# Block 1's attention with its projections in pieces of six matmuls between steps of heads, and values two steps later

## The chip, the cores and the metric

The kernel runs on one core of a Trainium2 chip. The time is in device microseconds (us), the median of several runs. Five engines work side by side and wait for each other through semaphores: TensorE (PE in the profile; its weight loads are PEld), VectorE (DVE), ScalarE (ACT), GpSimd (POOL) and SyncE (SP), whose queue issues most of the DMAs. Each engine works through its own instructions in the order in which the program issues them; that order is fixed when the program is built.

## The reference

Three blocks follow each other on x, 512 tokens by 1024 features. The change is in the first block's token mixing (`first_block`). All of it is float32.

```python
h = rms_norm(x, mix_norm)
qa, ka, va, qb, kb, vb = split(h @ w_in)      # 512, 512, 512, 512, 128, 128 columns
# 8 differential heads, each with two queries and two keys of 32, a value of 64
p  = softmax(q1 @ k1.T * scale + bias) - lam * softmax(q2 @ k2.T * scale + bias)
oa = rms_norm(p @ va, diff_subln) * (1 - lambda_init)
# 8 grouped heads of 64; 4 share a key and a value
qb, kb = rope(rms_norm(qb, q_norm)), rope(rms_norm(kb, k_norm))
ob = softmax(qb @ kb.T * 64 ** -0.5) @ vb
x  = x + concat(oa, ob) @ w_out
```

## The kernel before, in words

**Layout.** Activations stand feature-major: a chunk is 128 features (partitions) by 512 tokens. float32 products are made from three matmuls of fp32r operands: each operand is split into a high part and a low part, and high by high, low by high and high by low are accumulated (lines 120 to 122, `mm3x`). A projection onto one chunk sums over eight input chunks, so it is 24 matmuls of 128x512. Its weight arrives by DMA (`wraw`, line 169); ACT makes the high part (`whi`, line 137) and DVE, or POOL where `pool_lo` is set, the low part (`wlo`, line 138).

**Banks.** The eight PSUM banks are letters a to h. Scores use a and b, transposed weights of the softmax c and d, outputs e and f; small sums and turns use g ("st"), and a projection made during the heads uses h ("pj").

**The attention (`heads1`, from line 563).** There are four q chunks and four k chunks of the differential heads, four q chunks and one k chunk (called chunk 4) of the grouped heads. A q or k chunk is scaled out of its bank (`af`, line 607), split by ACT and DVE into one buffer `hl` (`parts`, lines 488 to 500; `HL` is the number of its buffers), and written to DRAM (line 499: `qdd`, `kdd`, `qpd`, `kpd`). The operands of a head are then loaded back from there in the row order that a score matmul needs (`qd` and `kd`, line 614; `qg`, line 690; `kg`, line 598). The grouped ones go through a norm and rope first (`rope`, lines 569 to 591): sums over features on PE, small operations of DVE, a rotation on ACT and POOL (lines 583 to 585), a copy `hr` of the norm on POOL (line 242), which PE turns into bank g (line 247), and a product on DVE.

**Values.** `v_tokens` (line 505) makes all values at once with tokens on the partitions: 192 matmuls of 128x320 in four banks, c to f.

**Heads.** Sixteen heads are run in the order differential, grouped, differential, grouped, with two of each per chunk. `attend` emits, for each of four chunks of 128 queries of a head, the scores (two matmuls for the two softmaxes, line 627, or two that add up, line 651), the softmax (a biased minimum or a minimum on DVE, lines 629 and 652; an exponential on ACT, line 485), the sum of the two softmaxes (lines 635 to 641; chunks 0 and 2 on POOL, lines 638 and 639), and the values of the *previous* head (`values`: four transposes, line 462, a split by ACT and DVE, lines 470 and 471, two matmuls, lines 472 and 473).

**What sets the order.** Before the heads stand seven projections (k chunk 4 of the grouped heads; q, k and grouped q of chunks 0 and 1) and the values. When a head's first score is built (`lazy`, `mk_diff`, `mk_gqa`), the projections and operand loads that belong there are emitted. Engine priority is by emission, and `issue_after(x)` holds an instruction behind x. `half_res` adds the first half of the output projection, eight pieces of twelve matmuls, held behind marks of the last heads (`M0`, `M1`); after the attention comes the other half.

Of the kernel before, what the change touches and what calls it, by code (L numbers as in the profile page):

```python
# [29 lines left out]
def f32v(ap):  # L30
    return ap.bitcast(F32)


class K:
    NU = 5
    SECOND = ("dq", "pf", "ct", "cacc")
    out = "out"
    NL = 4
    AH = 2
    HL = 1  # L40
# [14 lines left out]
    BANKS = {"mm": "abcdef", "scores": "ab", "abh": "abh", "e": "e", "fh": "fh", "turned": "cd", "out": "ef", "pj": "h", "cdef": "cdef", "st": "g", "bg": "h", "abcd": "abcd", "ef": "ef"}  # L55
# [375 lines left out]
    def attend(self, heads):  # L431

        nc = self.nc
        pv, self.marks = None, []
        for unit, vt, odd, dst, done in heads + [(None,) * 5]:
            ps_, fin = [], None
            for q in range(4):
                f = unit(q) if unit else None  # L440
                if fin:
                    ps_.append(fin())
                fin = f
                if pv:
                    self.values(pv, q)
            if fin:
                ps_.append(fin())
            if pv:
                self.fold(pv[0], pv[3], pv[4])
                if pv[5]:  # L450
                    pv[5]()
            pv = [None, ps_, vt, odd, dst, done] if unit else None
# [52 lines left out]
    def v_tokens(self, src, xhl, vt, rtok, nh):  # L505

        nc = self.nc
        for half in range(2):
            pv = [self.psum("cdef") for _ in range(4)]
            for k0, kn in ((0, 3), (3, 3), (6, 2)):  # L510
                W = self.weight(src[half][:, k0 * 320:(k0 + kn) * 320], kn * 320, kn)
                for q in range(4):
                    s = slice(q * 128, (q + 1) * 128)
                    self.mm3x(pv[q][:, :320], [(xhl[k0 + k][0][:, s], xhl[k0 + k][1][:, s]) + W[k] for k in range(kn)], k0 == 0, k0 == 6)
            for q in range(4):
                hv = vt[q][:, half * 5:half * 5 + 5]
                pvv = pv[q][:, :320].rearrange("p (h d) -> p h d", h=5)
                nc.scalar.activation(hv[:, :, 0:64], pvv, AF.Copy, scale=rtok[:, q:q + 1])
                nc.vector.scalar_tensor_tensor(out=hv[:, :, 64:128], in0=pvv, scalar=rtok[:, q:q + 1], in1=f32v(hv[:, :, 0:64]), op0=ALU.mult, op1=ALU.subtract)

    def mix1(self, inp, gnext):
# [7 lines left out]
        with self.phase("att"):  # L529
            self.heads1(xhl, rb, rtok, gq, ind, ocs)  # L530
            part = self.half_res(ocs, gs, res)
# [15 lines left out]
    def half_res(self, ocs, gs, res):  # L547

        nc, D = self.nc, self.D
        ohl = self.o_parts(ocs, gs, (0, 4, 1, 5), "x", 16)  # L550
        part = self.dr.tile([8, 128, 512], F32, name="part")
        for c in range(8):
            x = self.keep("xa", 3)
            nc.sync.dma_start(out=x, in_=res[c])
            self.pool_lo = self.PA
            with self.tc.issue_after(self.marks[32 + self.M0 + self.M1 * c // 8]):
                p = self.proj(D["w_out"][c][:, :512], ohl, 4, "pj")
            self.pool_lo = False
            nc.vector.tensor_add(x, p, x)
            nc.sync.dma_start(out=part[c], in_=x)  # L560
        return part

    def heads1(self, xhl, rb, rtok, gq, ind, ocs):
# [5 lines left out]
        def rope(c, name, kind="pj"):  # L569
# [5 lines left out]
            nc.vector.tensor_mul(f0, self.proj(D["w1_in"][8 + c], xhl, kind=kind), rb)  # L575
# [13 lines left out]
            return self.parts(f, name)  # L589

        d = rope(4, "kpd", "mm")

        def keys(kv):
            ds = []
            for i in range(2):
                t = self.keep("kg", 2, F32R)
                for r in range(2):
                    nc.sync.dma_start(out=f32v(t[64 * r:64 * r + 64]), in_=self.part_rows(d, i, 32 * kv, [(64, 2), (1, 32)]))
# [18 lines left out]
        def diff_head(h, sms, q2, k2):  # L617
# [4 lines left out]
            def unit(q):  # L622
                mx = self.small("mx", 2, 4)
                es = []
                for s in range(2):
                    p = self.psum("scores")
                    nc.tensor.matmul(p, q2[:96, s, q * 128:(q + 1) * 128], k2[:96, s], start=True, stop=True)
# [29 lines left out]
        qds, kds, qgd = {}, {}, {}  # L657
# [10 lines left out]
        def proj_q(c, kind="pj"):  # L668
            qds[c] = scaled("qdd", self.proj(D["w1_in"][c], xhl, kind=kind), -(32 ** -0.5))

        def proj_k(c, kind="pj"):
            kds[c] = scaled("kdd", self.proj(D["w1_in"][4 + c], xhl, kind=kind), 1.0)

        def mk_diff(c, r):
            if r == 1:
                qgd[c + self.AH] = rope(c + self.AH, "qpd") if c < 4 - self.AH else None
# [1434 lines left out]
```

## Time and profile before

| what | us |
|---|---|
| median of 3 runs (2668.03, 2668.23, 2671.92) | 2668.23 |
| profiled execution | 2667.55 |
| its span, first to last instruction | 2665.6 |
| attention stage, from the sixth projection's end (422.83) to the output projection's second half (671.90) | 249.07 |
| first score matmul | 450.24 |

The profile is of one execution. Its mean granted TensorE clock is 0.989 of full speed. In the table of engines a busy time and its share stand with the number of instructions. In the views by windows each row is a stretch of the span in us, with the busy time of each engine and the number of its instructions. In timelines a row has start, duration, engine, line, operation, output <- inputs, and in brackets the idle time ahead of the instruction with what ended it. Matmuls are pipelined, so that the distance of two starts, not the duration, is what one costs.

### The profile page before, as it was taken

What the parts mean: (1) busy time and instruction counts of PE and PEld (TensorE: products, weight loads), DVE (VectorE), ACT (ScalarE), POOL (GpSimd) and SP (SyncE); (2) the same over time, 40 slices, a digit from 0 to 9 for tenths busy, and PEclk for the clock granted to TensorE, in tenths of its full rate; (3) what the DMA queues carried; (4) which work ended last, traced back from release to release, by engine and by line L of the source; (5) the groups of instructions that cost most, each with busy time, mean ns of one, the idle gap of its engine ahead of it and who ended that gap; (6) DMA issues with size and microseconds to landing.
All of it is one profiled execution on the core that took longest, in us unless ns stands there. A gap on an engine that the chain in (4) does not pass through costs nothing.

```text
span 2665.6 us, 31162 instructions
## 1 busy us (share of the span) xinstructions
PE 2590.5 (97%) x11804; PEld 2093.0 (79%) x11804; DVE 1580.7 (59%) x2446; ACT 1052.8 (39%) x1621; POOL 405.0 (15%) x331
## 2 busy tenths in 40 slices
PE   8999998989999999999999999999899899999999
PEld 6887787767788887988788777888788777878787
DVE  7876645888644544567435854334545976746564
ACT  4222233776422324555323533223433463424242
POOL 1011012233000003133112201001200313101000
PEclk9999999999999999999999999999999999999999
DMA  5565644433632234432223343222524644322323
GB/s 197 179 200 189 212 154 128 152 111 103 208 96 96 87 103 134 143 106 70 97 95 134 127 144 99 95 95 95 186 70 147 211 103 156 95 94 91 100 87 111
DMA packets 114593, 339.99 MB, mean 128 GB/s; under 512 B 13784, under 2 KB 15768, under 8 KB 114314
## 3 DMA queue, kind: packets, MB, share of 16 engines
q1 hardware_dynamic: 104010, 301.02, 34.6%
q0 software_dynamic: 10432, 36.97, 4.4%
q8 instruction: 92, 1.51, 0.2%
q14 instruction: 59, 0.48, 0.1%
HBM read 301.47 MB, written 40.67 MB: 128 GB/s over the span
## 4 chain that ended last, share of the span: by engine, by line
PE 78%; issue 8%; DVE 6%; DMA 4%; ACT 2%; POOL 1%; SPq 0%; POOLq 0%; ACTq 0%; DVEq 0%
PE a L121 4%; PE a L120 4%; PE a L122 4%; PE e L122 4%; PE c L122 4%; PE c L121 4%; PE c L120 4%; PE e L120 4%; PE e L121 4%; PE b L122 4%; PE f L120 4%; PE f L121 4%; PE b L120 4%; PE b L121 4%; PE f L122 4%
## 5 line engine op out<-in xcount | busy, mean ns | idle before, releaser
L137 ACT ACTIVATE whi<-wraw 128x1024 fp32r<-128x1024 f32 (+4 forms) x420 | 423.9, 1012 | 1024.9 <-PE e L121 169.6
L138 DVE TENSOR_TENSOR wlo<-wraw,whi 128x1024 fp32r<-128x1024 f32 (+5 forms) x408 | 492.3, 1209 | 323.1 <-ACT whi L137 317.4
L122 PE MATMUL e<-xh,wlo 128*128 128x512 f32 x368 | 144.0, 391 | 1.6 <-DVE wlo L138 1.6
L120 PE MATMUL e<-xh,whi 128*128 128x512 f32 x368 | 144.2, 392 | 0.0
L121 PE MATMUL e<-xl,whi 128*128 128x512 f32 x368 | 144.1, 392 | 0.0
L121 PE MATMUL a<-xl,whi 128*128 128x512 f32 x352 | 139.2, 396 | 2.4 <-DVE xl L194 2.0
L120 PE MATMUL a<-xh,whi 128*128 128x512 f32 x352 | 138.9, 395 | 0.2 <-ACT xh L897 0.2
L122 PE MATMUL a<-xh,wlo 128*128 128x512 f32 x352 | 138.1, 392 | 0.1
L121 PE MATMUL c<-xl,whi 128*128 128x512 f32 x344 | 135.3, 393 | 2.5 <-DVE xl L194 2.5
L120 PE MATMUL c<-xh,whi 128*128 128x512 f32 x344 | 135.7, 394 | 0.0
L122 PE MATMUL c<-xh,wlo 128*128 128x512 f32 x344 | 135.1, 393 | 0.0
L120 PE MATMUL b<-xh,whi 128*128 128x512 f32 x304 | 120.2, 395 | 10.1 <-ACT xh L193 7.7
L121 PE MATMUL b<-xl,whi 128*128 128x512 f32 x304 | 120.2, 395 | 0.0
L122 PE MATMUL b<-xh,wlo 128*128 128x512 f32 x304 | 119.8, 394 | 0.3 <-DVE wlo L138 0.3
L190 ACT ACTIVATE hh<-h 128x512 fp32r<-128x512 f32 x98 | 61.8, 630 | 144.6 <-DVE h L369 93.0
L928 POOL TENSOR_TENSOR acc<-sq 128x512 f32<-128x512 f32 x10 | 14.1, 1406 | 638.3 <-ACT sq L296 371.8
L122 PE MATMUL f<-xh,wlo 128*128 128x512 f32 x280 | 109.8, 392 | 0.6 <-DVE wlo L138 0.6
L120 PE MATMUL f<-xh,whi 128*128 128x512 f32 x280 | 110.2, 394 | 0.0
L121 PE MATMUL f<-xl,whi 128*128 128x512 f32 x280 | 109.4, 391 | 0.0
L122 PE MATMUL d<-xh,wlo 128*128 128x512 f32 x264 | 104.2, 395 | 1.6 <-DVE wlo L138 1.6
L120 PE MATMUL d<-xh,whi 128*128 128x512 f32 x264 | 104.3, 395 | 0.0
L121 PE MATMUL d<-xl,whi 128*128 128x512 f32 x264 | 103.7, 393 | 0.0
(1181 smaller groups left out, 6447.2 us busy)
## 6 DMA issues: line engine op xcount, KB each, us to landing
wraw<-w_up SPq DMA_DIRECT2D x76, 512.0 KB
mw<-w_mod POOLq DMA_DIRECT2D x48, 512.0 KB, 4.6
wraw<-ffn_w_gate SPq DMA_DIRECT2D x43, 512.0 KB
wraw<-ffn_w_up SPq DMA_DIRECT2D x43, 512.0 KB
wraw<-w_down SPq DMA_DIRECT2D x40, 512.0 KB
wraw<-ffn_w_down SPq DMA_DIRECT2D x32, 448.0 KB
wraw<-w_gate SPq DMA_DIRECT2D x24, 512.0 KB
wraw<-ffn_w_down SPq DMA_DIRECT2D x16, 512.0 KB
```

Source lines behind the costliest of these rows:

```text
L120: mm(out, ah, bh, start=(first and i == 0), stop=False)
L121: mm(out, ah, bl, start=False, stop=False)
L122: self.last_mm = mm(out, al, bh, start=False, stop=(last and i == n - 1)).ins
L137: nc.scalar.activation(hi[:, i:j], raw[:, i:j], AF.Copy)
L138: (nc.gpsimd if self.pool_lo else nc.vector).tensor_sub(lo[:, i:j], raw[:, i:j], f32v(hi[:, i:j]))
L190: nc.scalar.activation(hi, x, AF.Copy)
L928: i = (self.nc.vector if c == 6 else self.nc.gpsimd).tensor_add(a, acc, s).ins
```

## The change

`attend` is given `fill`, a generator, and `lag`. It emits in steps: one query chunk of one head (scores, softmax), then the values of the chunk that was emitted 4 + `lag` steps earlier (`lag` is 2 here, so six steps; before, four), then one piece of `fill`. A piece is six matmuls: two of the eight input chunks of a projection (`proj_pieces`). A projection takes four steps. `fill` goes through chunks 1 to 3, each with grouped q (rope), q, k and v, and then through the first half of the output projection (two pieces each).

Values are now four chunks and a fifth for the grouped heads, made feature-major like every other projection; each is scaled on DVE, turned by four PE transposes into bank g and split there (`turn_v`).

Ahead of the heads stand six projections: q0, k0, grouped q 0, chunk 4, v0 and v4. The loads of the first head's operands come right behind k0. Operands of a head are loaded one head ahead (`ahead_diff`, `ahead_gqa`). There are two `hl` buffers, four operand buffers in place of three, and three of `kg` in place of two. `pool_lo` is set for all of `fill`, so that POOL makes the low parts of its twelve full weights too. The third block's attention uses the same `attend` without fill and lag, with its own counter of score banks.

```diff
-    AH = 2
-    HL = 1
+    HL = 2
...
-    M0 = 4
-    M1 = 30
-    PA = True
...
+    def attend(self, heads, fill=None, lag=0):
+
+
+
+
+        n, pvs, fin, self.marks = len(heads), [], None, []
+        for step in range(4 * n + 4 + lag):
+            f, (h, q) = None, divmod(step, 4)
+            if h < n:
+                unit, vt, odd, dst, done = heads[h]
+                if q == 0:
+                    pvs.append([None, [], vt, odd, dst, done])
+                f = unit(q)
...
+                fin[0].append(fin[1]())
+            fin = (pvs[h][1], f) if f else None
+            h, kc = divmod(step - 4 - lag, 4)
+            if h >= 0:
+                pv = pvs[h]
+                self.values(pv, kc)
+                if kc == 3:
+                    self.fold(pv[0], pv[3], pv[4])
+                    if pv[5]:
+                        pv[5]()
+            if fill:
+                with self.tc.issue_after(self.marks[-1] if self.marks else self.last_score):
+                    next(fill, None)
...
+    def proj_pieces(self, src, xhl, evac, kind="pj"):
+
+        W = self.weight(src, 1024, 8)
+        p = self.psum(kind)
+        for k in range(0, 8, 2):
+            self.mm3x(p, [W[k] + xhl[k], W[k + 1] + xhl[k + 1]], k == 0, k == 6)
+            if k == 6:
+                evac(p)
+            yield
...
-            self.pool_lo = self.PA
-            with self.tc.issue_after(self.marks[32 + self.M0 + self.M1 * c // 8]):
-                p = self.proj(D["w_out"][c][:, :512], ohl, 4, "pj")
...
+            W = self.weight(D["w_out"][c][:, :512], 512, 4)
+            p = self.psum("pj")
+            for k in range(0, 4, 2):
+                self.mm3x(p, [W[k] + ohl[k], W[k + 1] + ohl[k + 1]], k == 0, k == 2)
+                if k == 2:
+                    nc.vector.tensor_add(x, p, x)
+                    nc.sync.dma_start(out=part[c], in_=x)
+                yield
...
-                t = self.keep("kg", 2, F32R)
+                t = self.keep("kg", 3, F32R)
...
-        vt = [self.keep("vt", 4, F32R, w=1280).rearrange("p (h d) -> p h d", h=10) for _ in range(4)]
...
+        vt = [self.keep("vt", 5, F32R, w=1024).rearrange("p (q h d) -> p q h d", q=4, h=2) for _ in range(5)]
+
+        def turn_v(p, c):
+            f = self.t("vf")
+            nc.vector.tensor_mul(f, p, rb)
+            p = self.psum("st")
+            for q in range(4):
+                nc.tensor.transpose(p[:, q * 128:q * 128 + 128], f[:, q * 128:q * 128 + 128], self.ident)
+            p = p.rearrange("p (q h d) -> p q h d", q=4, h=2)
+            nc.scalar.activation(vt[c][:, :, :, 0:64], p, AF.Copy)
+            nc.vector.tensor_sub(vt[c][:, :, :, 64:128], p, f32v(vt[c][:, :, :, 0:64]))
...
-            t = self.keep(tag, 3, F32R, tag="op1", w=1024).rearrange("p (r w) -> p r w", r=2)
+            t = self.keep(tag, 4, F32R, tag="op1", w=1024).rearrange("p (r w) -> p r w", r=2)
...
-                    nc.tensor.matmul(p, q2[:96, s, q * 128:(q + 1) * 128], k2[:96, s], start=True, stop=True)
+                    self.last_score = nc.tensor.matmul(p, q2[:96, s, q * 128:(q + 1) * 128], k2[:96, s], start=True, stop=True).ins
...
+        def chunk(kind, c):
+
+            return {"q": (D["w1_in"][c], lambda p: scaled(qds, c, "qdd", p, -(32 ** -0.5))),
+                    "k": (D["w1_in"][4 + c], lambda p: scaled(kds, c, "kdd", p, 1.0)),
+                    "g": (D["w1_in"][8 + c], lambda p: rope(p, c)),
+                    "v": (D["w1_v"][c], lambda p: turn_v(p, c))}[kind]
+
+        def ahead_diff(c, r):
+
+            ops[c, r] = operand("qd", qds[c], r, (0, 0, 1)), operand("kd", kds[c], r, (0, 1, 0))
+
+        def ahead_gqa(c, r):
+            if r == 0 and c % 2 == 0:
+                kg[c // 2] = keys(c // 2)
...
+            ops[4 + c, r] = t
+
+        def mk_diff(c, r):
+            ahead_gqa(c, r)
+            return diff_head(2 * c + r, sms[c], *ops[c, r])
+
+        def mk_gqa(c, r):
+            if (c, r) != (3, 1):
+                ahead_diff(c + r, 1 - r)
+            return gqa_head(r, sms[4 + c], ops[4 + c, r], kg[c // 2])
...
-        for c in range(self.AH):
-            proj_q(c, "mm")
-            proj_k(c, "mm")
-            qgd[c] = rope(c, "qpd", "mm")
+        for kind, c in (("q", 0), ("k", 0), ("g", 0), ("g", 4), ("v", 0), ("v", 4)):
+            src, evac = chunk(kind, c)
+            evac(self.proj(src, xhl))
+            if kind == "k":
+                ahead_diff(0, 0)
+
+        def fill():
+            self.pool_lo = True
+            for c in range(1, 4):
+                for kind in "gqkv":
+                    yield from self.proj_pieces(*chunk(kind, c)[:1], xhl, chunk(kind, c)[1])
+            yield from rest()
+            self.pool_lo = False
...
-        self.attend(heads)
+                heads.append((lazy(lambda c=c, r=r: mk_diff(c, r)), [vt[c][:, q, r] for q in range(4)], r, ocs[c], normed(c) if r else None))
+                heads.append((lazy(lambda c=c, r=r: mk_gqa(c, r)), [vt[4][:, q, h // 4] for q in range(4)], r, ocs[4 + c], normed(4 + c) if r else None))
+        self.attend(heads, fill(), 2)
...
-    A["w1_v"] = moving(np.concatenate([w[:, 1024:1536], w[:, 2176:]], 1), 320)
+    A["w1_v"] = panels(np.concatenate([w[:, 1024:1536], w[:, 2176:]], 1))
```

**PE, at the start of the scores.** Rows of PE's order, of before; `kd` and `qd` are the operands of the first differential head, `f_3459` a bank of the values (the fourth of the first half), `c_3456` to `e_3458` the three others. Words in a row are the line, the operation, output<-inputs and the shape.

```order
L122 MATMUL f_3459<-whi_3462,xl_2750 128x320
L120 MATMUL f_3459<-whi_3504,xh_2788 128x320
L121 MATMUL f_3459<-wlo_3505,xh_2788 128x320
L122 MATMUL f_3459<-whi_3504,xl_2789 128x320
L120 MATMUL f_3459<-whi_3504,xh_2827 128x320
L627 MATMUL a_3395<-kd_3388,qd_3384 128x512
L220 MATMUL g_3343<-vecs_74,sq_3344 128x2 x4
L627 MATMUL b_3400<-kd_3388,qd_3384 128x512
L121 MATMUL f_3459<-wlo_3505,xh_2827 128x320
L122 MATMUL f_3459<-whi_3504,xl_2828 128x320
L120 MATMUL f_3459<-whi_3504,xh_2866 128x320
L121 MATMUL f_3459<-wlo_3505,xh_2866 128x320
```

The same place in the changed kernel: `f_3290` is the sixth projection (v4), `h_3352` the first piece of grouped q of chunk 1. The lines have moved with the edits: 120 to 122 are 116 to 118 now, 242 is 238, 462 is 463, 499 is 500, 614 is 618, 627 is 631, 638 and 639 are 642 and 643.

```order
L117 MATMUL f_3290<-xl_2945,whi_3286 128x512
L118 MATMUL f_3290<-xh_2944,wlo_3287 128x512
L631 MATMUL a_3336<-kd_3092,qd_3088 128x512
L631 MATMUL b_3341<-kd_3092,qd_3088 128x512
L116 MATMUL h_3352<-xh_2673,whi_3348 128x512
L117 MATMUL h_3352<-xl_2674,whi_3348 128x512
L118 MATMUL h_3352<-xh_2673,wlo_3349 128x512
L116 MATMUL h_3352<-xh_2710,whi_3348 128x512
L117 MATMUL h_3352<-xl_2711,whi_3348 128x512
L118 MATMUL h_3352<-xh_2710,wlo_3349 128x512
L631 MATMUL a_3360<-kd_3092,qd_3088 128x512
L631 MATMUL b_3365<-kd_3092,qd_3088 128x512
```

Scores now stand directly behind the last of six projections, with one piece of six matmuls between two steps; before, they stood among the value matmuls, behind seven projections and most of the first half of the values.

**POOL, around the first grouped head.** Of before: `rot` and `hr` belong to rope, `e1` to the sums of two softmaxes.

```order
L242 COPY hr_3219<-rr_3203 128x4x64 x2
L584 TENSOR_TENSOR rot_3364<-rot_3364,rope_2996 128x512
L585 TENSOR_TENSOR rot_3364<-ra_3362,rot_3364 128x512
L242 COPY hr_3369<-rr_3353 128x4x64 x2
L638 TENSOR_SCALAR e1_3402<-e1_3402,rs_3416 128x512
L639 TENSOR_TENSOR e1_3402<-e1_3402,e0_3397 128x512
L638 TENSOR_SCALAR e1_3429<-e1_3429,rs_3447 128x512
L639 TENSOR_TENSOR e1_3429<-e1_3429,e0_3424 128x512
L638 TENSOR_SCALAR e1_3958<-e1_3958,rs_3984 128x512
L639 TENSOR_TENSOR e1_3958<-e1_3958,e0_3953 128x512
```

Of the changed kernel: `e1_3343` and `e1_3389` are the sums of chunks 0 and 2 of the first head, `wlo_3598` the low half of the weight of k of chunk 1, `hr_3229` the norm of the grouped keys (chunk 4).

```order
L580 TENSOR_TENSOR rot_3224<-rot_3224,rope_2997 128x512
L581 TENSOR_TENSOR rot_3224<-ra_3222,rot_3224 128x512
L642 TENSOR_SCALAR e1_3343<-e1_3343,rs_3370 128x512
L643 TENSOR_TENSOR e1_3343<-e1_3343,e0_3338 128x512
L642 TENSOR_SCALAR e1_3389<-e1_3389,rs_3413 128x512
L134 TENSOR_TENSOR wlo_3598<-wraw_3595,whi_3597 128x1024
L238 COPY hr_3229<-rr_3213 128x4x64 x2
L643 TENSOR_TENSOR e1_3389<-e1_3389,e0_3384 128x512
L580 TENSOR_TENSOR rot_3447<-rot_3447,rope_2997 128x512
L581 TENSOR_TENSOR rot_3447<-ra_3445,rot_3447 128x512
```

The low half now stands between two halves of a head's work and the copy of the grouped keys' norm. This is where PE stands in the changed kernel at that place (`c_3520` and `d_3544` are the transposed weights of the first head's values, `g_3232` the turned norm, `g_3277` the turned v4):

```order
L117 MATMUL h_3352<-xl_2945,whi_3348 128x512
L118 MATMUL h_3352<-xh_2944,wlo_3349 128x512
L463 MATMUL c_3520<-ident_72,e1_3343 128x128
L463 MATMUL c_3520<-ident_72,e1_3367 128x128
L463 MATMUL d_3544<-ident_72,e1_3343 128x128
L463 MATMUL d_3544<-ident_72,e1_3367 128x128
L243 MATMUL g_3232<-ident_72,hr_3229 128x128 x4
L463 MATMUL c_3520<-ident_72,e1_3389 128x128
L463 MATMUL c_3520<-ident_72,e1_3410 128x128
L463 MATMUL d_3544<-ident_72,e1_3389 128x128
L463 MATMUL d_3544<-ident_72,e1_3410 128x128
L604 MATMUL g_3277<-ident_72,vf_3275 128x128 x4
```

PE needs `e1_3343`, then `hr_3229`, then `e1_3389`, in the order in which POOL makes them, with the low half ahead of `hr_3229`.

**SP's queue, at a change of chunk.** Of before, from the write of k of chunk 2 (`kdd_3788`) on; its first load stands seven rows below the last one shown:

```order
L499 DMA kdd_3788<-hl_3785 128x1024
L169 DMA wraw_5722<-w_out 128x512
L614 DMA kd_4172<-kdd_3308 32x2x512 x3
L614 DMA qd_4523<-qdd_3270 32x2x512 x3
L620 DMA btab_4531<-be2_2029 128x896
L169 DMA wraw_5745<-w_out 128x512
L690 DMA qg_4640<-qpd_3382 64x1x512 x2
L499 DMA qpd_3938<-hl_3935 128x1024
L614 DMA kd_4527<-kdd_3308 32x2x512 x3
L614 DMA qd_4751<-qdd_3750 32x2x512 x3
```

Of the changed kernel, the change from chunk 1 to chunk 2 (`kdd_4335` is the write of k of chunk 2, `kd_4341` the load of its first half for the head that follows):

```order
L500 DMA qpd_4054<-hl_4051 128x1024
L500 DMA qdd_4189<-hl_4186 128x1024
L688 DMA qg_4468<-qpd_4054 64x1x512 x2
L618 DMA qd_4337<-qdd_4189 32x2x512 x3
L624 DMA btab_4823<-be2_2029 128x896
L500 DMA kdd_4335<-hl_4332 128x1024
L165 DMA wraw_4996<-w1_v 128x1024
L618 DMA kd_4341<-kdd_4335 32x2x512 x3
L618 DMA qd_4685<-qdd_4189 32x2x512 x3
L592 DMA kg_4465<-kpd_3242 64x1x512 x2
L618 DMA kd_4689<-kdd_4335 32x2x512 x3
```

The write of the keys and their load now stand one behind the other with a weight load between them; before, writes stood several rows ahead of the loads that need them.

More of the change, by code (lines that the diff above doesn't have):

```diff
@@ L54 @@
     NW = 3
-    BANKS = {"mm": "abcdef", "scores": "ab", "abh": "abh", "e": "e", "fh": "fh", "turned": "cd", "out": "ef", "pj": "h", "cdef": "cdef", "st": "g", "bg": "h", "abcd": "abcd", "ef": "ef"}
+    BANKS = {"mm": "abcdef", "scores": "ab", "scores3": "ab", "abh": "abh", "e": "e", "fh": "fh", "turned": "cd", "out": "ef", "pj": "h", "cdef": "cdef", "st": "g", "bg": "h", "abcd": "abcd", "ef": "ef"}
     def __init__(self, ctx, tc, D):
@@ L503, in part_rows @@
         return bass.AP(tensor=d.tensor, offset=d.offset + row * 1024 + part * 512, ap=[[s * 1024, n] for s, n in dims] + [[1, 512]])
[L505 to L519, printed above, removed]
+    def proj_pieces(self, src, xhl, evac, kind="pj"):
[6 more added lines that the diff above has]
+            yield
     def mix1(self, inp, gnext):
@@ L529, in mix1 @@
         with self.phase("att"):
-            self.heads1(xhl, rb, rtok, gq, ind, ocs)
-            part = self.half_res(ocs, gs, res)
+            part = self.dr.tile([8, 128, 512], F32, name="part")
+            self.heads1(xhl, rb, gq, ind, ocs, lambda: self.half_res(ocs, gs, res, part))
         with self.phase("wo"):
@@ L554, in half_res, with heads1 @@
             nc.sync.dma_start(out=x, in_=res[c])
-            self.pool_lo = self.PA
-            with self.tc.issue_after(self.marks[32 + self.M0 + self.M1 * c // 8]):
-                p = self.proj(D["w_out"][c][:, :512], ohl, 4, "pj")
[L558 to L563, printed above, removed]
+            W = self.weight(D["w_out"][c][:, :512], 512, 4)
[6 more added lines that the diff above has]
+                yield
+    def heads1(self, xhl, rb, gq, ind, ocs, rest):
         nc, D = self.nc, self.D
@@ L567, in heads1, with rope @@
         nc.sync.dma_start(out=cs, in_=D["rope1"])
-        def rope(c, name, kind="pj"):
+        def rope(p, c):
             i = int(c == 4)
             f0 = self.t("rf0")
-            nc.vector.tensor_mul(f0, self.proj(D["w1_in"][8 + c], xhl, kind=kind), rb)
+            nc.vector.tensor_mul(f0, p, rb)
             st = self.psum("st")
@@ L588, in rope @@
             nc.vector.scalar_tensor_tensor(out=f, in0=p, scalar=1.0 if c == 4 else -0.125, in1=rot, op0=ALU.mult, op1=ALU.mult)
-            return self.parts(f, name)
-        d = rope(4, "kpd", "mm")
+            gds[c] = self.parts(f, "kpd" if c == 4 else "qpd")
         def keys(kv):
@@ L655, in gqa_head @@
             return unit
-        qds, kds, qgd = {}, {}, {}
+        qds, kds, gds, ops = {}, {}, {}, {}
         def lazy(mk):
@@ L666, in lazy @@
             return unit
[L668 to L676, printed above, removed]
-            return diff_head(2 * c + r, sms[c], operand("qd", qds[c], r, (0, 0, 1)), operand("kd", kds[c], r, (0, 1, 0)))
-        def mk_gqa(c, r):
-            if r == 0:
-                if c == 0:
-                    self.v_tokens(D["w1_v"], xhl, vt, rtok, 5)
-                if c % 2 == 0:
-                    kg[c // 2] = keys(c // 2)
-                if c < 4 - self.AH:
-                    proj_q(c + self.AH)
-                    proj_k(c + self.AH)
+        def chunk(kind, c):
[8 more added lines that the diff above has]
+                kg[c // 2] = keys(c // 2)
             t = self.keep("qg", 2, F32R)
             for i in range(2):
-                nc.sync.dma_start(out=f32v(t[64 * i:64 * i + 64]), in_=self.part_rows(qgd[c], i, 32 * r, [(64, 2), (1, 32)]))
-            return gqa_head(r, sms[4 + c], t, kg[c // 2])
+                nc.sync.dma_start(out=f32v(t[64 * i:64 * i + 64]), in_=self.part_rows(gds[c], i, 32 * r, [(64, 2), (1, 32)]))
+            ops[4 + c, r] = t
[6 more added lines that the diff above has]
+            return gqa_head(r, sms[4 + c], ops[4 + c, r], kg[c // 2])
         kg = {}
```

31 lines of the change are left out of this document (5 added, 26 removed).

## The prediction

> **What bounds the kernel now.** The page's first part comes first: TensorE is busy nearly all the time, so only work taken from it, time in which it waits, and time at a lower clock can be won.
>
> ```profile
> span 2665.6 us, 31162 instructions
> PE 2590.5 (97%) x11804; PEld 2093.0 (79%) x11804; DVE 1580.7 (59%) x2446; ACT 1052.8 (39%) x1621; POOL 405.0 (15%) x331
> ```
>
> The change touches one stage. The view by windows shows it from the end of the sixth projection (422.83) to the first matmul behind the attention (671.90); the first row is the dense matmuls ahead of it.
>
> ```profile
> core 0: us, PE busy (x) PEld busy (x) DVE busy (x) ACT busy (x) POOL busy (x), PEclk, DMA share, GB/s
> 388.60:422.83 34.23, 34.23 (x168) 28.72 (x167) 13.78 (x29) 9.76 (x14) 4.18 (x4) 1.00 0.41 138
> 422.83:450.24 27.41, 18.87 (x104) 17.14 (x103) 10.60 (x18) 6.79 (x10) 4.16 (x4) 0.91 0.49 154
> 520.00:600.00 80.00, 68.98 (x337) 50.30 (x336) 66.81 (x179) 57.89 (x135) 29.28 (x22) 0.89 0.36 113
> 600.00:671.90 71.90, 68.68 (x388) 50.92 (x386) 59.23 (x142) 48.64 (x109) 21.05 (x15) 1.00 0.36 116
> 390.00:672.00 282.00, 257.12 (x1344) 203.07 (x1342) 205.10 (x485) 168.40 (x360) 78.48 (x60) 0.95 0.41 132
> ```
>
> From 390 to 672 PE idles 282 − 257.12 = 24.9 us. The clock averages 0.95, so about 0.05 × 282 = 14.1 us more go to slow matmuls. The stage itself is 671.90 − 422.83 = 249.07 us, so its PE work at full clock is about 249.1 − 24.9 − 14.1 = 210.1. **The prize is at most 39 us, 1.5% of the run.** The view of waits (from 422 to 672) names the two largest:
>
> ```profile
> engine line waited for: us in total, times, longest us
> PE a L627 <- DMA qd<-qdd: 5.7, 1, 5.7
> PE a L627 <- DMA kd<-kdd: 3.9, 1, 3.9
> ```
>
> The slow clock follows short idles, as the timeline of PE shows: after 0.86 us of idle the instructions behind start 0.60 us apart, where 128x512 matmuls in a dense stretch start 0.2267 us apart (three of them lie from 422.15 to 422.83).
>
> ```profile
> 523.34 0.50 PE L627 MATMUL a<-kd,qd 96*128 96x512 f32 x1 [0.86 <-DVE mx L629]
> 523.94 0.80 PE L473 MATMUL f<-ptl,vt 128*128 128x512 f32 x1
> 524.54 0.63 PE L472 MATMUL f<-pth,vt 128*128 128x512 f32 x1
> ...
> 422.15 0.39 PE L120 MATMUL f<-xh,whi 128*128 128x512 f32 x1
> ...
> 422.83 0.39 PE L120 MATMUL a<-xh,whi 128*128 128x512 f32 x1
> ```
>
> By the Trainium skill ("TensorE: Matmul & The Clock Gate", section "HAM oscillation — how this bites in real kernels") only idle gaps above about 3.4 us slow the clock. By that rule the clock term below (1.5 us in the first grouped head, about 1 in each chunk change) would keep only the first part and the time would come out some 3 us lower; this trace disagrees, with its 0.86 us.
>
> **Why the start is late.** q0 and k0 are done long before the first score. The timelines of ACT, SyncE's queue and PE show why:
>
> ```profile
> 435.60 0.63 ACT L493 ACTIVATE hl<-af 128x512 fp32r<-128x512 f32 x1 [5.41 <-DMA qdd<-hl]
> 422.33 0.33 SPq L499 DMA_DIRECT2D kpd<-hl  x1
> 425.50 1.14 SPq L598 DMA_DIRECT2D kg<-kpd  x2
> 426.69 0.43 SPq L499 DMA_DIRECT2D qdd<-hl  x1
> 435.64 1.51 SPq L614 DMA_DIRECT2D qd<-qdd  x3
> 446.32 0.79 SPq L614 DMA_DIRECT2D kd<-kdd  x2
> 450.24 0.77 PE L627 MATMUL a<-kd,qd 96*128 96x512 f32 x1 [5.69 <-DMA qd<-qdd]
> ```
>
> There is one hl buffer: each projection's split waits on ACT until the write before it has landed. A write takes 425.50 − 422.33 = 3.2 us at best, 435.64 − 426.69 = 8.9 us beside a weight load. The loads behind it end by 450.24, at most 3.9 us after 446.32.
>
> **The change, part by part.**
>
> *Start.* q0 and k0 come first, their operand loads are issued ahead of the other four projections, and two hl buffers let both writes run at once. Four projections take 4 × 24 × 0.2267 = 21.8 us behind k0; eviction about 3 us, write and loads 7.1 to 12.8 us: the first score stands right behind the sixth projection, with about 6 us to spare. The 8.5 us idle of 422.83 to 450.24 and its slow clock go. This is counted by taking all of before's losses off and adding those that I expect after.
>
> *PE work.* v as 128x320 (192 matmuls) goes; five projections of 24 matmuls 128x512 come, with 20 transposes. Pitches from the timeline:
>
> ```profile
> 456.96 0.31 PE L122 MATMUL d<-whi,xl 128*128 128x320 f32 x1
> 457.11 0.31 PE L121 MATMUL e<-wlo,xh 128*128 128x320 f32 x1
> 457.26 0.31 PE L122 MATMUL e<-whi,xl 128*128 128x320 f32 x1
> ...
> 653.86 0.60 PE L462 MATMUL c<-ident,e 128*128 128x128 f32 x4
> 654.22 0.47 PE L120 MATMUL h<-xh,whi 128*128 128x512 f32 x1
> 654.53 0.39 PE L121 MATMUL h<-xl,whi 128*128 128x512 f32 x1
> ```
>
> 0.147 us for 320, 0.36 / 4 = 0.09 us for a transpose, and 0.31 instead of 0.23 for a piece's first matmul. So −192 × 0.147 = −28.2; + 120 × 0.2267 = +27.2; + 20 × 0.09 = +1.8; about 30 more entries into a piece × 0.08 = +2.4. **Work: 210.1 + 3.2 = 213.3 us.** One step (a 1.4 us piece, two or so score matmuls, four transposes, two value matmuls) is about 2.8 us.
>
> *First grouped head.* POOL now makes all twelve full low halves of the weights, and stands in line. Durations of its instructions in the stage, and of the 1024-wide low half on POOL (from the groups of the whole trace), and on DVE (there 1024 wide, and 960 for v):
>
> ```profile
> L638 POOL TENSOR_SCALAR e<-e,rs 128x512 f32<-128x512 f32 x16 | 25.4, 1587 | 84.1 <-DVE rs L636 39.5 <-ACT e L485 30.4 <-DVE rm L203 5.9
> L639 POOL TENSOR_TENSOR e<-e,e 128x512 f32<-128x512 f32 x16 | 23.3, 1457 | 1.3
> L242 POOL COPY hr<-rr 128x256 f32<-128x256 f32 x10 | 4.5, 481 | 8.4 <-DVE rr L211 8.4
> L138 POOL TENSOR_TENSOR wlo<-wraw,whi 128x1024 fp32r<-128x1024 f32 x4 | 9.6, 2408 | 6.5 <-ACT whi L137 6.5
> L138 DVE TENSOR_TENSOR wlo<-wraw,whi 128x1024 fp32r<-128x1024 f32 x11 | 13.6, 1234 | 11.3 <-ACT whi L137 11.3
> L138 DVE TENSOR_TENSOR wlo<-wraw,whi 128x960 fp32r<-128x960 f32 x4 | 4.6, 1157 | 0.8 <-ACT whi L137 0.8
> ```
>
> At the head's first transposes the new order has on POOL: the sum of chunk 0 (e1), e1's scaling for chunk 2 (1.59), a low half (2.41, whose high half waits until PE has left the first fill projection), two hr copies (0.96), the sum of chunk 2 (1.46). PE needs the first sum, then hr (the turn of g4's norm), then the second sum. An estimate along that row: 1.2 until the first sum, then 1.59 + 2.41 + 0.96 − 0.4 for four transposes = 4.6, then 1.46 − 0.4 = 1.0, then 0.7 until the turned v is let into bank g, which DVE first must read: 7.5 idle (between 0, if POOL is far ahead, and 12), with 1.5 for the clock: **9.0**.
>
> *kpd.* The grouped keys hang on the same hr: read, split and written about 2.4 us later, landing after 3.2 to 8.9, loaded within 3.9. They are in place 6.2 + 2.4 + 3.2 + 3.9 = 15.7 to 21.4 us after the first fill projection; PE's work and waits up to the first grouped score are about 15. Wait 0.7 to 6.4; I take **3.5**. The SyncE queue has a weight load ahead of that write, which itself waits for POOL's low half.
>
> *Chunk changes* (three). Keys of the next chunk are complete four steps before they are used: 4 × 2.8 = 11.2 us. They need eviction and split, about 4 us in queues on DVE and ACT, a write of 3.2 to 8.9, and loads of 3.9 to 8.6. The upper end of the loads is before's one case of that kind:
>
> ```profile
> 579.07 1.27 SPq L614 DMA_DIRECT2D kd<-kdd  x3
> 587.66 0.47 PE L627 MATMUL a<-kd,qd 96*128 96x512 f32 x1 [3.90 <-DMA kd<-kdd]
> ```
>
> 11.1 to 21.5 us against 11.2: a wait of 0 to 10.3. The DMAs are at 0.36 to 0.41 of their time in the stage, so I lean to the low side: 1.5 idle and 1 of clock, **3 × 2.5 = 7.5**.
>
> *DVE and POOL.* Of the thirteen projections before and the v weights DVE keeps six low halves: −7 × 1.23 − 4.6 = −13.2, and at most 5 × 2 × 0.69 = 6.9 back for reading five v out in two passes (0.69 is the shortest of L641 below). POOL gains 12 × 2.41 = 28.9 us. What a busy POOL costs shows in the shortest, median and longest of two DVE instructions, and in the mean of a third:
>
> ```profile
> L641 DVE SCALAR_TENSOR_TENSOR e<-e,rs,e x16: 694/751/1687, 469.8 to 645.6; 128x512 f32<-128x512 f32 x16
> L209 DVE TENSOR_TENSOR ru<-ry x16: 146/166/1233, 428.4 to 663.5; 128x8 f32<-128x8 f32 x16
> L636 DVE SCALAR_TENSOR_TENSOR rs<-rs,nlam,sums 128x1 f32<-128x1 f32 x32 | 9.2, 288 | 0.3
> ```
>
> The same instruction takes 0.15 or 1.23 us. The means of these groups lie above their medians or minima by some 9 us in all, with 78.5 us of POOL; 29 more, in longer pieces, make 3 to 7 us more of DVE time. Between nothing and 7 on PE I take **2**: DVE is busy 205 of 282, so most is covered, but not where a softmax ends last. The Trainium skill ("SBUF — State Buffer", section "Who interferes with whom") says that a DVE instruction with two SBUF inputs and a GpSimd instruction that reads SBUF shut each other out; the maxima above agree. It speaks against moving low halves to POOL, and is the third rival's mechanism.
>
> *The rest.* Grouped steps with a rope beside them are DVE's: **2.5**, by 520 to 600, where DVE was 66.8 of 80 busy and PE lost 11. The other steps lose at the rate of 600 to 671.9 (3.2 of 71.9, half of it in the end): **3.5**. The last six steps have no piece to cover the chain score, softmax, transpose, values: **2**.
>
> Sum of losses: 9 + 3.5 + 7.5 + 2 + 2.5 + 3.5 + 2 = 30. The stage takes 213.3 + 30 = 243.3 against 249.07: −5.8. The profiled run took 2667.55 (span 2665.6 and 1.95 around it), 0.7 under the median of 2668.23. 2667.55 − 5.8 = 2661.8: **2662 us**.
>
> **Rivals.**
>
> *The stalls find cover* (faster still). For it: two hl buffers and loads a head ahead; one hl row above alone shows ACT idle for 5.41 us. Then the first grouped head, kpd and chunk changes keep a third of 20 us: −13.3, **2649**. Against: POOL's order, which is fixed.
>
> *The keys come late at each chunk change* (slower). If write and load meet weight loads, with 8.9 and 3.9: 4 + 8.9 + 3.9 = 16.8 against 11.2, 5.6 idle and 1.6 of clock, 7.2 each, 21.6 instead of 7.5: +14, **2676**. It ends above before's range from about 6.2 per change. For it: the two longest waits of before are just of this kind, and the qdd write took 8.9. Against: two buffers, and fewer writes at once.
>
> *No change.* All 7 us of blocked DVE time land on PE (+5), or the first score waits some 4 us with its clock: **2667**.
>
> **How the numbers follow.** Forecast 0.44 (own range 2656 to 2667), cover 0.23, late keys 0.20, no change 0.13. A measurement of this kernel can tell about 0.2%, 5.3 us: faster means under 2663. That takes 0.6 of the forecast's case and the first rival: 0.50. Slower, over 2673.5: the second rival, 0.20. Same: 0.30. The range is from a little under the first rival to the second: 2646 to 2677.
>
> **What would show it.** The first a/b score directly behind the sixth projection, with no idle over 1 us. In the first grouped head, waits of PE on POOL's e and hr of 4 to 5 us, and on kg of a few. At heads 4, 8 and 12, waits on kd under 3 us (over 6: second rival). DVE's two-input groups with a higher mean, low halves at 2.4 us on POOL. PE idle from 390 to the end of the stage near 20 us with the clock at 0.96. The forecast fails if the rest of the program shifts, since I count it at nothing: its instructions keep their order but for bank numbers.

## The result and the profile after

The change made the kernel **slower**: median 2692.93 us (2691.14 to 2709.15, six runs) against 2667.60 for the kernel before in the same sessions, a ratio of 1.0105 (95% interval 1.0089 to 1.0121). The forecast of 2662 and its range of 2646 to 2677 missed it. The profiled execution took 2699.23 us, span 2697.5, so that it stands some 6 us above the median.

The first view is that of windows, over the same 330 us of both kernels (before, then after; columns as above):

```profile
390.00:720.00 330.00, 305.07 (x1562) 242.54 (x1561) 235.08 (x531) 190.80 (x393) 85.01 (x65) 0.96 0.44 146
```

```profile
390.00:720.00 330.00, 287.52 (x1361) 221.85 (x1361) 220.36 (x495) 182.00 (x377) 110.57 (x77) 0.92 0.39 123
```

PE idles 42.5 us where it idled 24.9: 17.6 us more, and the clock is 0.92 against 0.96. On average neither DVE nor the DMAs are short of time: DVE does less in the same time and the DMA share is lower. Only POOL does more (110.57 us in place of 85.01).

The spans differ by 31.9 us, and idle time and clock account for all of it. The clock that the traces record is 1 or 0.5, nothing between; at 0.5 matmuls of 128x512 start 0.43 us apart, in place of 0.23. Over the whole run PE idles 91.0 us in place of 75.1, which is 15.9 more. It is busy at 0.5 for 80.6 us in place of 49.1; half of the 31.5 us more, 15.8, is lost. PE's work itself, with its time at 0.5 counted as half, is the same: 2566.2 us, where it was 2565.9.

The view of waits of PE, after, from 380 to 720, shows what it waited for:

```profile
PE a L631 <- DMA qd<-qdd: 8.3, 2, 4.8
PE a L655 <- DMA kg<-kpd: 6.4, 2, 5.3
PE a L631 <- DMA kd<-kdd: 5.6, 1, 5.6
PE g L243 <- POOL hr L238: 5.3, 1, 5.3
PE a L116 <- ACT oh L189: 2.5, 2, 2.1
```

20.3 us are operands that come late from DRAM. Three rows of PE's timeline are the three changes of chunk; the first two rows are the start and the first grouped head:

```profile
419.22 0.40 PE L631 MATMUL a<-kd,qd 96*128 96x512 f32 x1
437.31 1.11 PE L243 MATMUL g<-ident,hr 128*128 128x128 f32 x4 [5.35 <-POOL hr L238]
...
498.84 0.77 PE L631 MATMUL a<-kd,qd 96*128 96x512 f32 x1 [5.59 <-DMA kd<-kdd]
559.84 0.77 PE L631 MATMUL a<-kd,qd 96*128 96x512 f32 x1 [3.42 <-DMA qd<-qdd]
625.16 0.76 PE L631 MATMUL a<-kd,qd 96*128 96x512 f32 x1 [4.85 <-DMA qd<-qdd]
```

The start went as forecast: the first score stands right behind the sixth projection, at 419.22 in place of 450.24, without a wait. What it won was lost again, and more.

Two suspects stand in the trace. One is POOL: at 480 a low half runs there, and beside it a DVE instruction that takes 0.69 us elsewhere takes 2.52, and the split of the keys behind it 1.77 (DVE and POOL of the timeline):

```profile
479.95 2.39 POOL L134 TENSOR_TENSOR wlo<-wraw,whi 128x1024 fp32r<-128x1024 f32 x1
482.30 1.74 POOL L643 TENSOR_TENSOR e<-e,e 128x512 f32<-128x512 f32 x1
480.37 2.52 DVE L645 SCALAR_TENSOR_TENSOR e<-e,rs,e 128x512 f32<-128x512 f32 x1
482.81 1.77 DVE L495 TENSOR_TENSOR hl<-af,hl 128x512 fp32r<-128x512 f32 x1
```

The other is the way over DRAM. SyncE's queue at the third change of chunk:

```profile
607.11 1.04 SPq L688 DMA_DIRECT2D qg<-qpd  x2
608.25 0.38 SPq L624 DMA_DIRECT2D btab<-be  x1
608.72 1.37 SPq L618 DMA_DIRECT2D qd<-qdd  x3
611.95 0.35 SPq L165 DMA_DIRECT2D wraw<-w_out  x1
612.51 0.34 SPq L500 DMA_DIRECT2D kdd<-hl  x1
621.34 0.79 SPq L618 DMA_DIRECT2D kd<-kdd  x2
```

The write of the keys takes 621.34 − 612.51 = 8.8 us for 512 KB, judged by the load that waits for it. The write of kpd in before, as large, took 3.2.

### The profile page after: what moved, and what is told of

It reads as the page before. It is cut to its first block, busy times and chain, and to the rows that moved or that the text cites. A ratio compares the mean times of both kernels' runs of the same rounds, so it can differ in the third digit from the quotient of the medians.

```text
span 2697.5 us, 31053 instructions
## 1 busy us (share of the span) xinstructions
PE 2606.5 (97%) x11752; PEld 2101.4 (78%) x11752; DVE 1579.3 (59%) x2435; ACT 1053.3 (39%) x1617; POOL 433.0 (16%) x343
## 4 chain that ended last, share of the span: by engine, by line
PE 87%; DVE 6%; DMA 4%; ACT 2%; issue 1%; POOL 0%; SPq 0%; DVEq 0%; POOLq 0%; ACTq 0%
PE b L118 5%; PE b L116 5%; PE b L117 5%; PE d L118 5%; PE d L116 5%; PE d L117 4%; PE f L116 4%; PE f L117 4%; PE f L118 4%; PE a L117 4%; PE a L118 4%; PE a L116 4%; PE c L116 4%; PE c L117 4%; PE c L118 4%; PE e L118 4%
## 5 line engine op out<-in xcount | busy, mean ns | idle before, releaser
L133 ACT ACTIVATE whi<-wraw 128x1024 fp32r<-128x1024 f32 (+3 forms) x419 | 423.7, 1014 | 1020.1 <-PE d L117 162.1
L134 DVE TENSOR_TENSOR wlo<-wraw,whi 128x1024 fp32r<-128x1024 f32 (+4 forms) x395 | 476.0, 1207 | 311.7 <-ACT whi L133 308.6
L118 PE MATMUL d<-xh,wlo 128*128 128x512 f32 x352 | 138.4, 393 | 2.0 <-DVE wlo L134 2.0
L116 PE MATMUL d<-xh,whi 128*128 128x512 f32 x352 | 138.6, 394 | 0.0
L117 PE MATMUL d<-xl,whi 128*128 128x512 f32 x352 | 138.0, 392 | 0.0
L945 POOL TENSOR_TENSOR acc<-sq 128x512 f32<-128x512 f32 x10 | 14.1, 1410 | 641.1 <-ACT sq L292 375.8
L118 PE MATMUL e<-xh,wlo 128*128 128x512 f32 x288 | 112.9, 392 | 1.6 <-DVE wlo L134 1.6
L116 PE MATMUL e<-xh,whi 128*128 128x512 f32 x288 | 112.9, 392 | 0.0
L117 PE MATMUL e<-xl,whi 128*128 128x512 f32 x288 | 112.8, 392 | 0.0
L117 PE MATMUL a<-xl,whi 128*128 128x512 f32 x280 | 110.7, 395 | 2.0 <-DVE xl L190 2.0
L116 PE MATMUL a<-xh,whi 128*128 128x512 f32 x280 | 110.9, 396 | 0.0
```

Source lines behind the costliest of these rows:

```text
L116: mm(out, ah, bh, start=(first and i == 0), stop=False)
L117: mm(out, ah, bl, start=False, stop=False)
L118: self.last_mm = mm(out, al, bh, start=False, stop=(last and i == n - 1)).ins
L133: nc.scalar.activation(hi[:, i:j], raw[:, i:j], AF.Copy)
L134: (nc.gpsimd if self.pool_lo else nc.vector).tensor_sub(lo[:, i:j], raw[:, i:j], f32v(hi[:, i:j]))
L945: i = (self.nc.vector if c == 6 else self.nc.gpsimd).tensor_add(a, acc, s).ins
```

## The experiments

All kernels were timed beside the kernel before on the same chip. That kernel's own median lay between 2667.6 and 2671.9 from set to set, so runs of different sets are compared by their ratios.

| run | kernel | median us | ratio to before, 95% interval |
|---|---|---|---|
| e1_dve_lo | after, low halves on DVE | 2716.06 | 1.0166 (1.0148 to 1.0184) |
| e2_keys_first | after, order k, q, g, v | 2695.07 | 1.0085 (1.0065 to 1.0104) |
| e3_both | both | 2690.53 | 1.0074 (1.0051 to 1.0096) |
| b1_two_hl | before, two hl buffers | 2681.36 | 1.0037 (1.0021 to 1.0052) |
| e4_spread | after, grouped loads spread | 2667.60 | 0.9991 (0.9981 to 1.0002) |
| b2_spread | before, grouped loads spread | 2671.27 | 1.0005 (0.9992 to 1.0018) |
| e5_spread_dve | e4 + e1 | 2671.81 | 1.0000 (0.9988 to 1.0013) |
| e6_spread_keys | e4 + e2 | 2660.93 | 0.9957 (0.9942 to 0.9973) |
| e7_hr_dve | e6, hr copied on DVE | 2661.74 | 0.9973 (0.9963 to 0.9983) |
| e8_lag0 | e6, values four steps behind | 2676.88 | 1.0025 (1.0013 to 1.0036) |
| e9_one_hl | e6, one hl buffer | 2661.28 | 0.9974 (0.9962 to 0.9987) |
| b3_two_hl_spread | b1 + spread | 2667.43 | 0.9991 (0.9979 to 1.0004) |
| e12_halved_few | after, halved loads | 2705.96 | 1.0125 (1.0107 to 1.0143) |
| e10_spread_qg | after, only qg spread | 2672.95 | 1.0003 (0.9992 to 1.0015) |
| e11_spread_kg | after, only kg spread | 2688.59 | 1.0057 (1.0037 to 1.0076) |

### POOL, or the keys?

```diff
 e1   def fill():
-            self.pool_lo = True
             for c in range(1, 4):
...
+            self.pool_lo = True
             yield from rest()
 e2
-                for kind in "gqkv":
+                for kind in "kqgv":
 b1 (on before)
-    HL = 1
+    HL = 2
```

> The changed kernel with the low halves of the twelve full weights back on DVE (POOL keeps only the eight of the output projection). Theory POOL: the low halves stand ahead of hr on POOL (PE waited 5.35 us there) and hold DVE instructions with two SBUF inputs (one took 2.52 us instead of 0.69 beside a low half, and the split of the keys came 2.9 us late). Then the wait on hr falls below 1.5 us, kg by about 3, each of the three waits at a change of chunk (5.6, 3.4, 4.9) by 2 to 3; some 16 us of idle and 5 of slow clock go: about 2672. Theory KEYS (the chain from k's projection over DRAM to the head is longer than its four steps anyway): only hr and kg shrink, the chunk waits stay at 3 to 6: about 2682. Theory DVE: its 14.8 us of added work land on PE: 2690 or more.

> The changed kernel with each chunk's projections in the order k, q, grouped q, v in place of grouped q, q, k, v; keys are complete twelve steps ahead of their use, not four. Theory KEYS: the three waits at a change of chunk (13.9 us of idle together) and their slow clock (about 6) go, the waits on hr and kg stay: about 2673. Theory POOL: blocked DVE and hr are what costs, so the time moves by less than 8 us: 2685 to 2693. If the grouped queries are now late (rope ends eight steps later), waits on qg of some us appear instead: 2685.

> Both edits at once. If POOL and KEYS are two separate causes, the gains of the two runs alone add up (about 2693 - 20 - 20 + up to 8 counted twice): 2653 to 2661. If both shorten the same chain, the sum is little better than the better of the two: 2670.

> The kernel before with two hl buffers in place of one, nothing else. If the one buffer is what held its start (ACT waited for the write of each split before the next one; PE idle 8.5 us between 422.83 and 450.24), the first score comes about 8 us earlier and the time falls to about 2658. If the first score then waits for the values or for weights instead, the time stays within 3 us of 2667.

In none of the four did a theory hold as it stood. e3 and b1 lie outside every time that was named. e1's time is one that theory DVE allowed and e2's, by its ratio (about 5 us under after), one that theory POOL did, but the traces show other reasons. With the low halves on DVE the wait on hr did fall (to 3.1 us), and the kernel is some 16 us slower still (the difference of the two ratios), since the operands came later: PE waits 24.2 us for kd, 13.0 for kg and 9.1 for qd. SyncE's queue of e1 at its second change of chunk, and a window of its views there:

```profile
553.72 1.04 SPq L688 DMA_DIRECT2D qg<-qpd  x2
554.97 1.26 SPq L618 DMA_DIRECT2D qd<-qdd  x3
556.57 1.18 SPq L592 DMA_DIRECT2D kg<-kpd  x2
557.79 5.56 SPq L688 DMA_DIRECT2D qg<-qpd  x2
563.46 2.53 SPq L500 DMA_DIRECT2D kdd<-hl  x1
...
576.36 1.26 SPq L618 DMA_DIRECT2D kd<-kdd  x3
```

```profile
569.00:575.00 6.00, 0.00 (x0) 0.00 (x0) 0.00 (x0) 0.00 (x0) 0.00 (x0) 0.56 0.23 85
```

Six loads of qg and kg stand ahead of the write of the keys, and it takes 12.9 us. From 569 to 575 PE, DVE, ACT and POOL all sit idle, and the DMAs are at 0.23 of their time: on average nothing is short of bandwidth, and yet everything waits. With keys first the waits on kd and qd went, but 14.3 us of waits on qg came. In before, two hl buffers brought the first writes closer to the loads of kg, and kd was late by 11.3 us. In each case the late transfer stands behind loads of qg or kg, or is one.

Stretches like this stand in the changed kernel too, in the view by windows:

```profile
447.00:453.00 6.00, 1.24 (x6) 0.67 (x4) 1.29 (x2) 0.51 (x2) 0.00 (x0) 1.00 0.13 45
616.00:621.00 5.00, 3.33 (x15) 2.11 (x13) 3.02 (x6) 2.52 (x6) 0.00 (x0) 1.00 0.12 48
```

A share of 0.12 to 0.13 of sixteen engines is two engines. The trace's record of single DMA packets bears this out: at 293 of 300 moments between 447 and 453 exactly two packets are under way, of 2,048 bytes and 84 ns each. A load of 128 KB at 48 GB/s takes 2.7 us, two of them 5.5, the four of a kg pair 11. The Trainium skill ("DMA: Bandwidth & Descriptors", section "Why a DMA increments its semaphore by 16 and not by 1") says that a DMA is split over as many engines, at most 16, as divide the slowest dimension that isn't 1 on both sides, and that such a transfer takes the lowest-numbered ones. The loads of qg and kg read two runs of 32 rows from DRAM, so that dimension is 2. The share and the two packets agree; which two engines they are is not in the trace.

The packets also show how such loads hold a write that comes behind them. The write of the keys at the first change of chunk and the weight load behind it (issued at 484.62 and 485.00) are packets of 4,096 bytes. From 485.6 to 488.4 mostly fourteen of these are under way and two of 2,048. From 489.8 to 491.3 only two are left, both of 4,096, and the load of the keys is issued at 491.40: no other engine has a packet left, and the load waits for these two. In before the end of the qdd write looks the same: from 432.5 to 435.4 two packets are under way at a time, first of 2,048 bytes, then of 4,096.

### Few DMA engines

```diff
-                for r in range(2):
-                    nc.sync.dma_start(out=f32v(t[64 * r:64 * r + 64]), in_=self.part_rows(gds[4], i, 32 * kv, [(64, 2), (1, 32)]))
+                for r in range(4):
+                    nc.sync.dma_start(out=f32v(t[32 * r:32 * r + 32]), in_=self.part_rows(gds[4], i, 32 * kv + 64 * (r % 2), [(1, 32)]))
```

and the same for qg: twice as many loads, each of 32 rows, the same bytes.

> The changed kernel; each load of grouped operands (qg, kg: 64 partitions, in DRAM two runs of 32 rows) is issued as two loads of 32 rows, so that its outermost dimension is 32 and not 2. Bytes and order stay. Theory FEW: these loads run on few of the 16 DMA engines (the view of DMAs shows stretches of 48 to 55 GB/s at a tenth of the engines' time, and four of 128 KB at 50 GB/s are 10.5 us, which is as long as the stretch), and the writes and loads that follow in the same queue finish only behind them. Then the stretches go, the writes of qdd, kdd and kpd land within 5 us (6.5 to 8.8 now), the waits on kg (6.4) and at the changes of chunk (13.9) fall below 7 together, and with the slow clock behind them the time goes to 2665 to 2675. Theory WEIGHTS (writes are slow because 512 KB weight loads run beside them): waits stay above 15 together, 2687 or more.

> The kernel before with the same edit of the loads. Theory FEW: the write of qdd behind four kg loads (8.9 us) lands in about 4, kd at head 2 of chunk 1 (3.9 us of wait) is in time, and the time falls from 2668 to about 2655. Theory WEIGHTS: within 3 us of 2668.

> The changed kernel with spread loads and the low halves of the twelve full weights on DVE. With DMAs out of the way this asks again what POOL's low halves cost. If they cost what the trace shows beside them (hr 5.35 us, keys' split held 2.9 us), it is 5 to 10 us faster than the spread kernel; if not, DVE's added work makes it the same or slower.

> The changed kernel with spread loads and the order k, q, grouped q, v. If the chain over DRAM is short enough once the loads are spread, the order matters little: within 5 us of the spread kernel. If keys four steps ahead are too late even so, it is 5 to 12 us faster than it, and waits on qg (14.3 us in the run without spread loads) stay under 4.

The theory of few engines held in the changed kernel: e4 takes back all that the change had lost (1.0105 to 0.9991). No wait on kg, qd or kd is left among PE's waits; the write of the keys lands in 477.74 − 474.75 = 3.0 us, with a weight load issued right behind it. SyncE's queue and the window of e4:

```profile
474.75 0.34 SPq L500 DMA_DIRECT2D kdd<-hl  x1
475.18 0.38 SPq L165 DMA_DIRECT2D wraw<-w_v  x1
475.65 0.74 SPq L688 DMA_DIRECT2D qg<-qpd  x1
477.74 1.27 SPq L618 DMA_DIRECT2D kd<-kdd  x3
```

```profile
390.00:720.00 330.00, 308.66 (x1508) 241.70 (x1509) 242.83 (x523) 192.27 (x392) 110.83 (x77) 0.95 0.45 143
```

Idle time fell from 42.5 to 21.3 us, the span by 31.5: each us of wait carried about half a us of slow clock behind it. (These are the two profiled executions; the medians differ by 25 us.) The same count over the whole run gives 21.2 us of idle time and 9.7 of clock, since PE is busy at 0.5 for 61.3 us here and for 80.6 in after. The weights as the cause are out in the changed kernel.

In before the edit is worth nothing, where the theory had named 2655: its two waits on DMAs (9.6 us) go, but the clock falls from 0.96 to 0.94 in the same window and idle time only from 24.9 to 19.7:

```profile
390.00:720.00 330.00, 310.27 (x1564) 244.80 (x1563) 237.38 (x531) 191.82 (x394) 83.71 (x65) 0.94 0.45 146
```

Over the whole run PE is busy at 0.5 for 68.9 us in place of 49.1, which costs 9.9 us; idle time falls by 5.4. Why the clock fell there is open.

With the DMAs out of the way the low halves on DVE (e5) are not faster, so POOL's part is small; and keys first (e6) is 7 us faster than e4. **e6 is faster than before (by 0.4%) and after.** The reason expected, keys that come too late, is not it: e4 has no wait on keys left, and PE idles 69.8 us in its whole run and 69.4 in e6's. What differs is the clock: PE is busy at 0.5 for 61.3 us in e4 and for 41.5 in e6, worth 9.9 us, and the spans of these two executions differ by 9.7. Why the clock is better there is open too.

### Is it the engines, and which loads?

e12 issues as many loads as e4, each of half the columns, but over both runs of rows: `in_=self.part_rows(...)[:, :, w]` with `w` a half. e10 and e11 spread one of the two kinds.

> The changed kernel; each load of qg and kg is issued as two of 256 columns each, over the same 64 partitions, so that there are as many loads, as small, as in the spread kernel, but the outermost dimension in DRAM stays 2. Theory FEW: nothing is won; stretches near 50 GB/s stay, the waits on kg, qd and kd stay above 15 us together, 2688 to 2705. Theory SMALLER (half the size or twice the number is what helped): as the spread kernel, 2664 to 2671.

> The changed kernel with only the loads of qg spread over 32 rows. If the qg loads (two to four of them stand in the queue ahead of each chunk's keys) hold the chunk changes, the waits on qd and kd (13.9 us) fall below 5 and the wait on kg (6.4) stays: about 2675. If kg does it, little changes: above 2688.

> The changed kernel with only the loads of kg spread. The wait on kg shrinks from 6.4 to below 4, since qg's loads still stand ahead of it; the three chunk changes keep two or three of their waits (kg is loaded beside only one of them): about 2684. If kg is what holds them all: below 2675.

PE's waits on operands in e12, then in e10:

```profile
PE a L632 <- DMA kd<-kdd: 14.9, 3, 12.9
PE a L656 <- DMA kg<-kpd: 5.3, 1, 5.3
```

```profile
PE a L655 <- DMA kg<-kpd: 4.0, 2, 3.0
PE a L631 <- DMA kd<-kdd: 0.9, 1, 0.9
```

Smaller and more loads don't help: e12 is the slowest but one, and its longest wait on kd is 12.9 us. Two packets are still under way at 330 of 400 moments between 452 and 460. By the ratios spreading both brings 0.0114 (30 us), qg alone 0.0102 (27 us; the waits on qd and kd fall to 0.9 us, that on kg to 4.0), kg alone 0.0048 (13 us). The gains overlap, and it is mainly the loads of qg, which the change puts ahead of the keys.

### What the other parts are worth

```diff
 e7   if split:  for i in range(2):
-                nc.gpsimd.tensor_copy(e[...], ...)
+                nc.vector.tensor_copy(e[...], ...)
 e8
-        self.attend(heads, fill(), 2)
+        self.attend(heads, fill(), 0)
```

> The kernel with spread loads and keys first (2660.9), and rope's copy hr made on DVE in place of POOL, so that it no longer stands behind a low half. Theory POOL-ORDER: the wait of PE on hr (5.4 us) falls to 2 or less, and the half clock behind it goes too: 2652 to 2656. If what comes next in PE's order (the second sum of two softmaxes on POOL, or the load of the grouped keys) is late instead, the time stays within 3 us of 2661.

> The kernel with spread loads and keys first, with values four steps behind their scores and not six. If the two more steps cover the softmax's chain, PE waits on DVE's and ACT's splits and sums more often without them: 3 to 10 us slower (2664 to 2671). If four steps were enough, within 3 us of 2661.

> The kernel with spread loads and keys first, with one hl buffer in place of two. In the fill the splits stand four steps (some 12 us) apart and a write now lands in 3 to 4 us, so one buffer should cost little there; ahead of the heads q0 and k0 follow each other by 5.4 us. Within 3 us of 2661. If two buffers are what keeps ACT free, ACT idles before hl and PE waits appear: 5 us slower or more.

> The kernel before with two hl buffers and with spread loads. With two hl buffers alone it was 10 us slower, and kd was late by 11.3 us behind four loads of kg. Theory FEW: that wait goes, two hl buffers now bring the first score forward by about 8 us, and the time falls to 2655 to 2664. If the start is held by something else, 2667 to 2672.

e7 changes where PE waits, not how long the run takes. PE's waits of e6, then of e7:

```profile
PE g L243 <- POOL hr L238: 5.4, 1, 5.4
```

```profile
PE g L243 <- DVE rs L640: 3.7, 1, 3.7
PE b L655 <- ACT e L486: 2.7, 2, 2.2
```

The copy now waits its turn on DVE, and the 1.7 us won there come back at grouped scores (2.7 us of waits on ACT that e6 does not have). The lag of two steps is worth 15 us against e7 and e9 of the same set (e8), more than expected: without it PE waits 4.2 us before the transposes, 3.1 before a piece and more often for ACT's exponentials, and idle time in the window is 28.3 us in place of 20.3. Two hl buffers are worth nothing that can be told once the loads are spread (e9). In before they cost 10 us alone (b1) and nothing with spread loads (b3), where the wait on kd is 0.7 us and not 11.3; the first score came earlier, but the gain expected of it did not come.

## Why the prediction was wrong, by its own steps

- **Start: right.** First score behind the sixth projection, no idle.
- **PE work: close.** 3.2 us more forecast; with the time at 0.5 counted as half, PE's work grew by 0.3.
- **First grouped head: right in the main.** 7.5 us of idle forecast, 5.35 + 0.32 measured, at hr, with a low half just ahead of it on POOL. But without that low half 3.1 us of the wait stay (e5), so the order on POOL is only a part of it, and e5 and e7 show that little was to be won there.
- **kpd: the upper end.** 3.5 us taken; the wait at the first grouped score is 5.3, within its range of 0.7 to 6.4.
- **Chunk changes: the step that failed.** It read "The DMAs are at 0.36 to 0.41 of their time in the stage, so I lean to the low side", took 1.5 us of idle each, and measured 5.59, 3.42 and 4.85: 13.9 us, not 4.5. The share is a mean over sixteen engines; two of them were full, and the write, spread over all sixteen, was done only when those two were. The working had also put the 8.9 us of the qdd write down to "a weight load". Its own fence showed two loads of kg at 425.50, ahead of that write. The rival that keys come late had the right event and nearly its idle time (3 × 5.6 = 16.8 us), but the wrong cause, weight loads, and too little clock behind it.
- **Slow clock: the term that was off by most.** 1.5 us for the first head and 1 for each chunk change were counted, 4.5 in all. From 390 to 720 PE was busy at 0.5 for 50.4 us, which costs 25.2. (Of idle time the forecast counted the other 25.5 of its 30 us, and 42.5 came.) Spreading the loads takes a part of both away; in e4 the clock still costs 15.4 us in this window. The Trainium skill's bound of 3.4 us ("TensorE: Matmul & The Clock Gate", section "HAM oscillation — how this bites in real kernels") does not hold here: behind the 1.84 us of idle at 425.68 matmuls of 128x512 start 0.43 us apart until 429.44:

```profile
425.68 0.49 PE L631 MATMUL a<-kd,qd 96*128 96x512 f32 x1 [1.84 <-DVE mx L633]
...
427.31 0.63 PE L117 MATMUL h<-xl,whi 128*128 128x512 f32 x1
427.74 0.63 PE L118 MATMUL h<-xh,wlo 128*128 128x512 f32 x1
...
429.44 0.46 PE L631 MATMUL a<-kd,qd 96*128 96x512 f32 x1
```

- **DVE and POOL: right mechanism, small price.** The DVE sum beside POOL has a mean of 974 ns, where it was 831. But taking the low halves off POOL won nothing in any run.

With its loads spread, the change forecast at 2662 takes 2667.6: some 25 of the 31 us by which the forecast was off hang on these loads. The rest is clock more than idle time, and open.

## What to carry to other kernels

Look at the DMA share in the stretches where PE waits for a transfer: here a small, steady fraction (0.12 to 0.13) meant that two of the sixteen engines did all the work, and the later write that was spread over all of them ended behind it. A mean share far from 1 over a stage says nothing about such a queue. Before moving loads about, make each one's outermost dimension, on both sides, one that spreads over all engines. It pays only where the waits cost time: the same edit won nothing in before.

## What the runs showed that was not expected

- Taking the low halves off POOL (e1) made the kernel some 16 us slower. At its second change of chunk more loads of qg and kg stood ahead of the write of the keys. With the loads spread (e5) the same edit costs nothing that can be told.
- A slower clock can take back the whole of what a removed wait brings (b2_spread: 9.6 us of DMA waits gone, no change in time), and a better clock can bring as much as removed waits would (e6 against e4: idle time the same, 9.7 us of span).
- PEclk is recorded while PE idles too: e1 shows 0.56 in a window in which PE does nothing. The 14.1 us of slow clock that the prediction worked out from a mean therefore counts some idle time twice, though little: of 27.3 us at 0.5 from 390 to 720 in before PE was busy in 25.4.
